# Expert weights of an MoE block, loaded with four neighbouring rows for each partition

## The chip, the cores and the metric

The kernel runs on one core of a Trainium2 chip, as one program. The metric is the time of the program on the device in microseconds. The core's engines are PE (matrix products; PEld is its weight load), DVE (vector), ACT (scalar), POOL and SP, which here only issues DMA transfers. On-chip memory has 128 partitions; a load is described by how many bytes in a run it puts into each partition.

## What is computed

One block of a diffusion backbone, on 512 tokens of 1024 features (and 256 context tokens that only warm up a recurrence): a norm with adaptive shift and scale, two mixers side by side (a gated linear recurrence and a long-convolution head group), an output projection, and then the part that takes most of the time, a mixture of 32 experts with two experts for each token. Last comes a norm. Cut to what matters here:

```
mod = silu(c) @ w_ada + b_ada          # six rows of 1024: shift, scale, gate, twice
x   = x + g1 * (concat(rmsnorm(ya), rmsnorm(yb)) @ w_out)
h   = rmsnorm(x, norm2_g) * (1 + sc2) + sh2
g   = softmax(h @ w_rg + b_rg)         # 4 groups, the best one is taken
e   = softmax over the 8 experts of that group of (h @ w_re + b_re), the best 2
for e in 32 experts:                   # combine[:, e] is 0 for tokens without e
    y   = (silu(h @ w_gate[e]) * (h @ w_up[e])) @ w_down[e]   # 1024 -> 512 -> 1024
    out = out + combine[:, e] * y
x   = rmsnorm(x + g2 * out, final_g)
```

The weights w_gate and w_up of an expert are 1024 x 512 numbers of 4 bytes, w_down is 512 x 1024; each matrix is 2 MB.

## The kernel before, in words

The function `tile_block_kernel` doesn't issue instructions as it goes. Its calls are recorded in a `Recorder`, and for nearly the whole program a planner (`order`, `forward`, `backward`) sorts them before anything is issued: it simulates every engine with a cost for each instruction, takes the ready one of highest priority, and repeats this 24 times with priorities from the pass before. A transfer costs it `nbytes / RATE` with a rate of 386 bytes a nanosecond. So the order on all engines follows from the planned times of all of them, and a changed cost in one stage can change the order in another.

The work comes in stages. Until some 300 us the mixers and the modulation rows run (loads of w_ada, w_in, w_out; products on PE; scans and convolutions on DVE and ACT). From 300 to 358 us come the output projection, the second norm and the routing. For the routing each block of 128 tokens `r` of the residual `x2` is transposed in eight pieces of 128 features into `h2T`, and multiplied with the router's weights `wrA`. For the gather three bf16 tiles `xp[0..2]` are made, which together hold the fp32 value: a copy scaled by the norm's `rs`, the remainder `rem` (what the copy's rounding left), its copy, and the remainder of that. Blocks 0 and 1 get theirs in the loop over `r` (DVE, or ACT where the planner finds it sooner); blocks 2 and 3 after it, the first step on ACT.

Then the experts. They are ranked by their number of tokens. The list `CAPS` gives each rank a fixed number of rows (64, 64, 64, 192, 128, 128, 96, nine times 64, fifteen times 32, and 0 for the last; a loop behind takes what doesn't fit). 31 experts are loaded, the first three (`NPRE`) by their own number before the routing is known. Units pack up to 128 rows: one with two experts of 64, or four experts of 32 (a "quad"). The last unit is such a quad. In `expert_units` a unit gathers its rows by products with 0/1 matrices (bf16, on `xp`), scaled and shifted into `XT` with the features on the partitions, and then `product` multiplies with the gate, up and down weights in fp32; for a quad, four experts stand beside each other, each in 32 columns of the array. The gated result `sg` is transposed into `HT` (features on the partitions again) for the down product, whose two column halves of 512 (the last in two quarters, `LASTP`, in the last unit) are scattered back onto `x2`.

The weights come in 186 loads of 1 MB: for each expert six, gate, up and down (`m`), two halves each (`h`). All are issued by SP, in a fixed order (`chain`), into a ring of 16 buffers of 8 KB a partition (some lie in the "arena", some in "slots", so one tensor has both names in the trace). A load waits until the last product that reads the buffer's old content is done. `wpart` says what a load reads. Before, it is

```
w = w[:, 512 * h:512 * h + 512] if m == "d" else w[512 * h:512 * h + 512]
return w.rearrange("(k p) n -> p k n", p=128)
```

so partition p gets the rows p, 128 + p, 256 + p and 384 + p, each 512 numbers or 2 KB in a run: 512 runs a load. Half h of gate and up are 512 of the 1024 rows; half h of down are 512 of the 1024 columns, with all 512 rows. A product takes the features in the same order as the weight's rows: step k multiplies features 128k to 128k + 127.

Helpers at the top of the file issue all recorded instructions, so that in the trace nearly all of them have the line L565 or L572 (L1822 for the expert loads).

## Time and profile before

| | before |
|---|---|
| median of three runs | 866.7 us (864.5 to 866.82) |
| own time of the profiled execution | 867.37 us |
| span of the profiled execution | 865.6 us |
| PE busy | 798.3 us, 92% of the span |
| DVE, ACT busy | 493.2 us, 279.4 us |
| moved by DMA | 259.71 MB, mean 300 GB/s |
| share of the chain that ended last | PE 64%, DMA 6%, DVE 4% |

The span is what the profiler sees between the first and the last instruction; the program's own time has 1.8 us around it. A share of busy time is a mean over stages; the page also cuts the span into 40 slices, and there PE is near full from the second slice on to the last four, and DMA from 440 us on. A DMA share slightly above 1 means that all 16 engines are full. The list of DMA packets says which run lengths there are: 112966 of 118025 are shorter than 8 KB.

### The profile page before, as it was taken

What the parts mean: (1) busy time and instruction counts of PE and PEld (TensorE: products, weight loads), DVE (VectorE), ACT (ScalarE), POOL (GpSimd) and SP (SyncE); (2) the same over time, 40 slices, a digit from 0 to 9 for tenths busy, and PEclk for the clock granted to TensorE, in tenths of its full rate; (3) what the DMA queues carried; (4) which work ended last, traced back from release to release, by engine and by line L of the source; (5) the groups of instructions that cost most, each with busy time, mean ns of one, the idle gap of its engine ahead of it and who ended that gap; (6) DMA issues with size and microseconds to landing.
All of it is one profiled execution on the core that took longest, in us unless ns stands there. A gap on an engine that the chain in (4) does not pass through costs nothing.

```text
span 865.6 us, 13258 instructions
## 1 busy us (share of the span) xinstructions
PE 798.3 (92%) x5218; PEld 441.1 (51%) x5219; DVE 493.2 (57%) x966; ACT 279.4 (32%) x505; POOL 6.7 (1%) x16
## 2 busy tenths in 40 slices
PE   1969999999998999699999999999999999999774
PEld 0336653587887778553545344444643435345222
DVE  7999967999999988813332332342422144233215
ACT  4688387944353325511102011011110111011005
POOL 0000000000000000000000000000000000000002
PEclk9998999999999999799999999999999999999988
DMA  8953669425221495789899999999999999999993
GB/s 280 415 205 122 226 218 419 158 78 191 73 98 61 163 388 215 255 311 368 292 388 386 387 387 385 387 385 387 386 386 387 387 387 386 386 386 386 387 376 132
DMA packets 118025, 259.71 MB, mean 300 GB/s; under 512 B 6672, under 2 KB 11792, under 8 KB 112966
## 3 DMA queue, kind: packets, MB, share of 16 engines
q1 hardware_dynamic: 117942, 258.80, 81.5%
q8 instruction: 42, 0.69, 0.3%
q14 instruction: 25, 0.20, 0.1%
q10 hardware_dynamic: 16, 0.02, 0.0%
HBM read 252.49 MB, written 6.31 MB: 299 GB/s over the span
## 4 chain that ended last, share of the span: by engine, by line
PE 64%; DMA 6%; DVE 4%; ACT 1%; issue 0%; ACTq 0%; DVEq 0%
PE bank L565 64%; DMA arena<-in_w_up_dram 3%; DMA slot<-in_w_down_dram 2%; DVE arena L565 1%; DVE arena L572 1%; DVE slot L572 1%; DMA slot<-in_w_out_dram 1%; ACT slot L565 1%; DVE slot L565 0%; DVE R L565 0%; ACT arena L565 0%; ACT slot L572 0%; DVE fine L565 0%; DVE finy L565 0%; DVE he L565 0%
## 5 line engine op out<-in xcount | busy, mean ns | idle before, releaser
L565 PE MATMUL bank<-arena 128*64 128x512 f32 (+7 forms) x1314 | 301.3, 558 | 27.5 <-ACT arena L565 14.2
L565 PE MATMUL bank<-slot 128*128 128x512 f32 x968 | 258.6, 411 | 9.8 <-ACT arena L565 2.9
L565 PEld LDWEIGHTS bank<-slot 128*128 128x128 f32 x968 | 177.7, 190 | 91.1 <-issue 27.2
L565 PE MATMUL bank<-slot,arena 128*32 128x512 f32 (+2 forms) x1088 | 208.5, 598 | 4.7 <-DMA slot<-in_w_ada_dram 2.0
L565 PEld LDWEIGHTS bank<-arena 128*64 128x64 f32 (+4 forms) x1314 | 107.2, 139 | 160.0 <-issue 103.4
L565 DVE TENSOR_TENSOR arena<-arena,bank 128x512 f32<-128x512 f32 (+2 forms) x131 | 80.4, 664 | 135.3 <-PE bank L565 135.1
L572 DVE TENSOR_TENSOR arena<-arena 128x512 f32<-128x512 f32 (+3 forms) x139 | 116.6, 870 | 5.5 <-DMA arena<-in_w_dram 3.0
L565 ACT ACTIVATE arena<-bank 128x512 f32<-128x512 f32 (+1 forms) x62 | 36.0, 597 | 235.2 <-PE bank L565 233.3
L565 PEld LDWEIGHTS bank<-slot,arena 128*32 128x32 f32 (+1 forms) x1088 | 52.2, 119 | 97.9 <-issue 81.6
L565 PEld LDWEIGHTS <-slot 128*128 128x128 bf16 x1344 | 78.2, 99 | 27.2 <-issue 26.7
L565 PE MATMUL bank<-R,slot 128*128 128x128 bf16 x1344 | 86.5, 222 | 0.7 <-DVE R L565 0.6
L572 DVE TENSOR_SCALAR arena<-bank,A2c,B2c 128x128 f32<-128x128 f32 x42 | 16.8, 409 | 119.6 <-PE bank L565 119.5
L565 ACT ACTIVATE slot<-arena 128x512 fp32r<-128x512 f32 (+3 forms) x47 | 31.8, 679 | 108.0 <-DVE arena L565 95.5
L572 ACT ACTIVATE arena<-bank,B2c,A2c 128x128 f32<-128x128 f32 x70 | 28.1, 455 | 115.2 <-DVE arena L572 93.1
L565 DVE SCALAR_TENSOR_TENSOR arena<-bank,iw,arena 128x512 f32<-128x512 f32 (+1 forms) x29 | 21.2, 732 | 46.1 <-PE bank L565 45.9
L565 PE MATMUL bank<-ident,arena 128*128 128x128 f32 (+2 forms) x234 | 37.9, 281 | 5.6 <-DVE arena L565 4.3
L565 ACT ACTIVATE arena<-arena 128x512 f32<-128x512 f32 (+6 forms) x59 | 32.9, 591 | 22.1 <-DVE arena L565 16.9
L565 PEld LDWEIGHTS bank<-ident,arena 128*128 128x128 f32 (+2 forms) x234 | 29.5, 156 | 18.5 <-DVE arena L565 9.1
L572 ACT ACTIVATE slot<-slot 128x1024 fp32r<-128x1024 f32 (+1 forms) x33 | 27.6, 862 | 27.5 <-DVE slot L572 15.3
L572 DVE TENSOR_TENSOR slot<-slot 128x1024 fp32r<-128x1024 f32 (+1 forms) x36 | 34.7, 985 | 0.0
L565 ACT ACT_TABLE_LOAD x21 | 26.9, 1283 | 4.6 <-DMA arena<-in_pack_dram 4.2
L565 DVE TENSOR_TENSOR arena<-bank,arena 128x512 f32<-128x512 f32 (+1 forms) x42 | 27.5, 681 | 0.6 <-PE bank L565 0.5
(169 smaller groups left out, 388.9 us busy)
## 6 DMA issues: line engine op xcount, KB each, us to landing
slot<-in_w_gate_dram SPq DMA_DIRECT2D x34, 1024.0 KB, 13.8
arena<-in_w_down_dram SPq DMA_DIRECT2D x34, 1024.0 KB, 14.0
arena<-in_w_up_dram SPq DMA_DIRECT2D x32, 1024.0 KB, 14.0
slot<-in_w_up_dram SPq DMA_DIRECT2D x30, 1024.0 KB, 14.2
arena<-in_w_gate_dram SPq DMA_DIRECT2D x28, 1024.0 KB, 13.5
slot<-in_w_down_dram SPq DMA_DIRECT2D x27, 1024.0 KB, 14.2
slot<-in_w_ada_dram SPq DMA_DIRECT2D x24, 1024.0 KB, 8.4
slot<-in_w_in_dram SPq DMA_DIRECT2D x8, 1024.0 KB, 4.8
```

The lines of the kernel that those rows point to most:

```text
L565: return self.rec.add(self.name, lambda: f(*[real(v) for v in args], **{k: real(v) for k, v in kw.items()}), outs, ins, cost, **x)
L572: return cost, lambda: f(*[real(v) for v in args], **{k: real(v) for k, v in kw.items()}), port
```

## The change

`wpart` now reads four neighbouring rows for a partition, `"(p k) n -> p k n"` with k of 4. For gate and up these are 8 KB in a run: partition p gets the rows 4p to 4p + 3 of the half, in 128 runs a load. Step k of the product then takes the features k, k + 4, k + 8, ... of a half of 512, so all that brings features onto partitions counts by fours: the transposes of `x2`, of the modulation rows `mr` and of `sg` read every fourth column, `xp` and `rem` are written so that a plane's block holds every fourth feature (in two pieces of 512), and the norm's gain `n2` and the router's weights `wr` are packed accordingly. For down a half is now two of a partition's four rows, all 1024 columns wide, again 8 KB in a run, and no longer 512 columns: the tile is cut as `(k c n)` with two rows and two column halves, and `expert_units` takes row step k from half `k // 2`. Both loads of an expert's w_down are needed for its first column half, and both are read until its second. In the last group, whose last load comes in two pieces, the down loads keep column halves (`cols=True`), in runs of 2 KB. The planner gets 0.92 of the bytes for all loads with the long runs.

```diff
+    def fours(v):
+
+        return v.reshape(2, 128, 4, -1).transpose(1, 0, 2, 3).reshape(128, -1)
+
...
@@ -1106,7 +1110,8 @@
-            T.transpose(b[:, 128 * q:128 * q + 128], mr[:, 128 * q:128 * q + 128], ident)
+
+            T.transpose(b[:, 128 * q:128 * q + 128], mr[:, q::4] if g else mr[:, 128 * q:128 * q + 128], ident)
...
+    def four(v):
+        return v.rearrange("s (p q) -> s q p", q=4)
+
+    def fours(v):
+        return v.rearrange("s (q p) -> s q p", q=4)
...
-                    k = 4 * kb + q
-                    T.transpose(b[:, q * 128:(q + 1) * 128], x2[:, r, k * 128:(k + 1) * 128], ident)
+                    T.transpose(b[:, q * 128:(q + 1) * 128], x2[:, r, 512 * kb + q:512 * kb + 512:4], ident)
...
-            X.copy(xp[0][:, r], x2[:, r], scale=rs)
-            V.scalar_tensor_tensor(rem, x2[:, r], rs, xp[0][:, r], op0=OP.mult, op1=OP.subtract)
+            for j in range(2):
+                xj, pj = four(x2[:, r, 512 * j:512 * j + 512]), fours(xp[0][:, r, 512 * j:512 * j + 512])
+                X.copy(pj, xj, scale=rs)
+                V.scalar_tensor_tensor(fours(rem[:, 512 * j:512 * j + 512]), xj, rs, pj, op0=OP.mult, op1=OP.subtract)
...
-        S.activation(rem, x2[:, r], AF.Copy, scale=rss[r % 2])
+        for j in range(2):
+            js = slice(512 * j, 512 * j + 512)
+            S.activation(fours(rem[:, js]), four(x2[:, r, js]), AF.Copy, scale=rss[r % 2])
...
-    def wpart(m, h, w):
-
-        w = w[:, 512 * h:512 * h + 512] if m == "d" else w[512 * h:512 * h + 512]
-        return w.rearrange("(k p) n -> p k n", p=128)
+    def wpart(m, h, w, cols=False):
+
+        if m == "d":
+            w = w.rearrange("(p k) n -> p k n", k=4)
+            if cols:
+                return w[:, :, 512 * h:512 * h + 512]
+            return w[:, 2 * h:2 * h + 2].rearrange("p k (c n) -> p k c n", c=2)
+        return w[512 * h:512 * h + 512].rearrange("(p k) n -> p k n", k=4)
...
-                o = REC.add("SP", go, [dst[:, :, c0:c0 + cols]], [eid[0:1, s:s + 1]] if s >= NPRE else [],
-                            540 if new else 60, nbytes=2048 * cols)
+                    se = wpart(m, h, se, bool(pieces))
+                    return nc.sync.dma_start(out=dst.ap(), in_=se[:, :, c0:c0 + cols] if pieces else se)
+
+                o = REC.add("SP", go, [dst], [eid[0:1, s:s + 1]] if s >= NPRE else [], 540 if new else 60,
+                            nbytes=2048 * cols * (1.0 if pieces else 0.92))
...
-                T.transpose(b[:, q * n:q * n + n], sg[:n, q * 128:(q + 1) * 128], ident[:n, :n])
+                T.transpose(b[:, q * n:q * n + n], sg[:n, q::4], ident[:n, :n])
...
-                b = product(sub, "d", HT[j], [(k, k, h) for k in range(4)], c0, m)
+                b = product(sub, "d", HT[j], [(k, k, h) if last else (k, 2 * (k % 2) + h, k // 2) for k in range(4)], c0, m)
...
-                load(*t, LASTP if gi == len(groups) - 1 and t == todo[-1] and m == "d" else ((0, 512),))
+                load(*t, None if gi < len(groups) - 1 or m != "d" else LASTP if t == todo[-1] else ((0, 512),))
```

The order of the instructions on every engine is the planner's, and it changes throughout. Three places of it follow; in them L569, L576 and L1845 are the same helpers' lines after the change as L565, L572 and L1822 before.

On PE in the middle of the last unit, before the change: `128x512` products are scatters (`bank<-slot`) of the unit before, `32x512` ones are one expert's share of a product of the last quad.

```order
L565 MATMUL bank_73<-slot 128x512
L565 MATMUL bank_67<-slot 128x512
L565 MATMUL bank_68<-slot 128x512
L565 MATMUL bank_71<-arena 32x512
L565 MATMUL bank_70<-slot 128x512
L565 MATMUL bank_71<-arena 32x512
L565 MATMUL bank_67<-slot 128x512
L565 MATMUL bank_68<-slot 128x512
L565 MATMUL bank_74<-slot 128x512
L565 MATMUL bank_69<-slot 128x512
```

After the change, the same place:

```order
L569 MATMUL bank_69<-slot,arena 32x512 x8
L569 MATMUL bank_71<-slot 128x512
L569 MATMUL bank_74<-slot 128x512
L569 MATMUL bank_67<-slot 128x512
L569 MATMUL bank_72<-slot 128x512
L569 MATMUL bank_69<-slot,arena 32x512 x6
L569 MATMUL bank_69<-arena 32x512 x2
L569 LDWEIGHTS R_137
L569 MATMUL bank_70<-combP,R_137 32x3
L569 MATMUL bank_69<-arena 32x512 x14
```

Before, single 32-row products stand between the scatters; after, they come in runs of 8, 8 and 14 (`combP` belongs to the placing of a unit's rows).

On SP around 300 us, where the last loads of the mixers meet the first of the experts: `w_out` is the output projection's weights, `x` the tokens, `gd` a scratch tensor of the filters. Before:

```order
L565 DMA slot<-in_w_out_dram 128x2048
L565 DMA arena<-in_x_dram 128x1024 x2
L565 DMA slot<-in_w_out_dram 128x2048
L565 DMA arena<-in_x_dram 128x1024
L1822 DMA arena<-in_w_gate_dram 128x4x512 x2
L565 DMA arena<-in_x_dram 128x1024
```

And after:

```order
L569 DMA slot<-in_w_out_dram 128x2048
L569 DMA arena<-gd 128x4x256 x2
L569 DMA slot<-in_w_out_dram 128x2048
L569 DMA arena<-in_x_dram 128x1024 x3
L1845 DMA arena<-in_w_gate_dram 128x2048 x2
L569 DMA arena<-in_x_dram 128x1024
```

The pieces of `gd` now stand between the two halves of `w_out`, and three blocks of `x` in a row go ahead of the first expert loads.

On DVE in the second norm, where the planes of a block are made (`hy` is a block's 1/rms, `slot<-arena,hy` the scaled copy, `arena<-arena,hy,slot` the remainder). Before:

```order
L565 TENSOR_TENSOR hy_101<-hy_101,he_103 128x1
L565 TENSOR_TENSOR he_102<-he_102,hv_98 128x1
L572 TENSOR_SCALAR slot<-arena,hy_101 128x1024
L565 TENSOR_SCALAR he_102<-he_102 128x1
L565 SCALAR_TENSOR_TENSOR arena<-arena,hy_101,slot 128x1024
L565 SCALAR_TENSOR_TENSOR arena<-bank_72,rsby_126,arena 128x512
L565 TENSOR_TENSOR hy_100<-hy_100,he_102 128x1
L572 CAST slot<-arena 128x1024
```

And after:

```order
L569 TENSOR_TENSOR hy_101<-hy_101,he_103 128x1
L569 RECIPROCAL hy_100<-hy_100 128x1
L576 TENSOR_SCALAR slot<-arena,hy_101 128x512
L569 TENSOR_TENSOR he_102<-hy_100 128x1
L569 SCALAR_TENSOR_TENSOR arena<-arena,hy_101,slot 128x512
L569 SCALAR_TENSOR_TENSOR arena<-bank_68,rsby_126,arena 128x512
L569 TENSOR_TENSOR he_102<-he_102,hv_98 128x1
L569 SCALAR_TENSOR_TENSOR arena<-arena,hy_101,slot 128x512
L569 SCALAR_TENSOR_TENSOR arena<-bank_71,rsby_126,arena 128x512
L569 TENSOR_SCALAR he_102<-he_102 128x1
L569 TENSOR_TENSOR hss_97<-sx_129 128x1
```

One copy of 1024 features and one remainder of 1024 are now pieces of 512, and instructions of the other block and of the residual (`rsby`) stand between them.

## Rows read from the trace of the kernel before

**Rows 1.** the page, part 1: busy time, share and instructions of each engine
```profile
PE 798.3 (92%) x5218; PEld 441.1 (51%) x5219; DVE 493.2 (57%) x966; ACT 279.4 (32%) x505; POOL 6.7 (1%) x16
```

**Rows 2.** windows: length, busy us (instructions) of each engine, granted clock, DMA share, GB/s
```profile
200.00:300.00 100.00, 95.72 (x443) 79.17 (x443) 97.41 (x117) 40.44 (x63) 0.00 (x0) 1.00 0.32 110
440.00:600.00 160.00, 159.81 (x1181) 74.21 (x1183) 55.50 (x108) 21.34 (x43) 0.00 (x0) 1.00 1.05 386
600.00:800.00 200.00, 199.31 (x1657) 91.92 (x1653) 65.81 (x127) 27.06 (x55) 0.00 (x0) 1.00 1.05 386
806.00:850.00 44.00, 32.39 (x208) 10.72 (x209) 10.67 (x19) 5.98 (x13) 1.69 (x2) 0.92 0.94 345
```

**Rows 3.** the chain that ended last: start us, us, engine or transfer
```profile
358.80 75.03 PE bank L565 x603
...
810.78 14.01 DMA arena<-in_w_up_dram
824.84 4.94 PE bank L565 x21
...
843.81 6.29 PE bank L565 x60
```

**Rows 4.** waits of PE, 806 to 850 us: total us, times, longest
```profile
PE bank L565 <- DMA arena<-in_w_up_dram: 5.0, 3, 1.7
PE bank L565 <- DMA arena<-in_w_down_dram: 1.7, 1, 1.7
PE bank L565 <- DMA slot<-in_w_up_dram: 1.5, 1, 1.5
PE bank L565 <- DMA slot<-in_w_down_dram: 1.1, 1, 1.1
```

**Rows 5.** windows, five us in the last unit
```profile
825.00:830.00 5.00, 5.00 (x25) 1.02 (x22) 0.00 (x0) 0.00 (x0) 0.00 (x0) 0.50 1.05 387
```

**Rows 6.** windows in which w_ada and w_in are loaded
```profile
26.00:36.00 10.00, 9.45 (x42) 4.18 (x44) 9.94 (x17) 6.11 (x12) 0.00 (x0) 1.00 1.01 417
138.00:148.00 10.00, 9.24 (x50) 2.90 (x52) 5.53 (x8) 7.85 (x11) 0.00 (x0) 1.00 1.02 419
```

**Rows 7.** line L1822 (the expert loads): from issue to landing
```profile
DMA to landing us min/median/max: 5.3/14.0/15.8
```

**Rows 8.** timeline of SP, 715 to 740: start us, us, line, operation, count
```profile
722.24 9.68 SPq L1822 DMA_DIRECT2D arena<-in_w_gate_dram  x4
733.50 2.53 SPq L1822 DMA_DIRECT2D slot<-in_w_gate_dram  x2
```

**Rows 9.** timeline of PE, three places: x counts passes, two for an fp32 product
```profile
749.94 3.64 PE L565 MATMUL bank<-slot,arena 128*32 128x512 f32 x32
753.40 1.04 PE L565 MATMUL bank<-arena 128*32 128x512 f32 x8
...
802.42 1.04 PE L565 MATMUL bank<-arena 128*32 128x512 f32 x2
803.40 0.49 PE L565 MATMUL bank<-slot 128*128 128x512 f32 x1
```

**Rows 10.** timeline of DVE in the mixers, out<-in and their shapes
```profile
50.31 0.69 DVE L572 TENSOR_TENSOR slot<-arena,slot 128x512 fp32r<-128x512 f32 x1
...
75.86 1.14 DVE L572 TENSOR_TENSOR slot<-arena,slot 128x512 fp32r<-128x512 f32 x1
```

**Rows 11.** timeline of ACT in the mixers
```profile
48.49 0.68 ACT L572 ACTIVATE slot<-arena 128x512 fp32r<-128x512 f32 x1
...
75.63 1.19 ACT L572 ACTIVATE slot<-arena 128x512 fp32r<-128x512 f32 x1
```

**Rows 12.** timeline of DVE before the experts
```profile
339.07 0.75 DVE L572 TENSOR_SCALAR slot<-arena,hy 128x1024 bf16<-128x1024 f32 x1
...
339.85 1.28 DVE L565 SCALAR_TENSOR_TENSOR arena<-arena,hy,slot 128x1024 f32<-128x1024 f32 x1
```

**Rows 13.** timeline of ACT before the experts
```profile
350.58 2.19 ACT L565 ACTIVATE arena<-arena,hy 128x1024 f32<-128x1024 f32 x2 [1.01 <-DVE hy L565]
```

More of the change, by code (lines that the diff above doesn't have):

```diff
@@ L106, in lay @@
     wr = np.concatenate([i["w_rg"][0], i["w_re"][0], np.zeros((D, 28), np.float32)], axis=1)
-    small = {"c": cols(i["c"]), "cc": cols(i["c_ctx"]), "n1": cols(i["norm1_g"]), "n2": cols(i["norm2_g"]), "fb1": twice(i["filt_b1"].T),
+    small = {"c": cols(i["c"]), "cc": cols(i["c_ctx"]), "n1": cols(i["norm1_g"]), "n2": fours(i["norm2_g"].reshape(D, 1)), "fb1": twice(i["filt_b1"].T),
              "ff1": twice(i["filt_freq1"].T), "fb2": twice(i["filt_b2"].T), "ff2": twice(i["filt_freq2"].T), "fw1": i["filt_w1"][0],
@@ L111, in lay @@
              "cbw": cols(i["conv_b_w"]), "ga": cols(i["out_norm_a"]),
[L112 removed]
+             "gb": cols(i["out_norm_b"]), "wr": fours(wr),
              "brb": np.broadcast_to(np.concatenate([i["b_rg"], i["b_re"]], axis=1), (128, 36)),
@@ L1803, with load @@
     regs, chain, owner = {}, [], {}
-    def load(s, m, h, pieces=((0, 512),)):
+    def load(s, m, h, pieces=None):
         src = wsrc[m]
@@ L1810, in load @@
             nring[0] += 1
-            dst = t[:, :].rearrange("p (k n) -> p k n", k=4)
-            for c0, cols in pieces:
+            wt[s, m, h] = t.rearrange("p (k n) -> p k n", k=4), (nring[0] - 1) % NW
+            for c0, cols in pieces or ((0, 512),):
+                if m == "d" and not pieces:
+                    dst = t.rearrange("p (k c n) -> p k c n", k=2, c=2)
+                else:
+                    dst = wt[s, m, h][0][:, :, c0:c0 + cols]
                 new = s >= NPRE and s not in regs
@@ L1816, in load, with go @@
                     regs[s] = None
-                def go(dst=dst[:, :, c0:c0 + cols], c0=c0, cols=cols, new=new):
+                def go(dst=dst, c0=c0, cols=cols, new=new):
                     if new:
@@ L1821, in go @@
                     se = src[s] if s < NPRE else src[ds(regs[s], 1)].rearrange("o k n -> (o k) n")
-                    return nc.sync.dma_start(out=dst.ap(), in_=wpart(m, h, se)[:, :, c0:c0 + cols])
-                o = REC.add("SP", go, [dst[:, :, c0:c0 + cols]], [eid[0:1, s:s + 1]] if s >= NPRE else [],
-                            540 if new else 60, nbytes=2048 * cols)
+                    se = wpart(m, h, se, bool(pieces))
+                    return nc.sync.dma_start(out=dst.ap(), in_=se[:, :, c0:c0 + cols] if pieces else se)
+                o = REC.add("SP", go, [dst], [eid[0:1, s:s + 1]] if s >= NPRE else [], 540 if new else 60,
+                            nbytes=2048 * cols * (1.0 if pieces else 0.92))
                 if chain:
@@ L2011 @@
                     for h in range(2):
-                        t = ring[len(wo)].rearrange("p (k n) -> p k n", k=4)
+                        t = ring[len(wo)]
                         se = wsrc[m][ds(e, 1)].rearrange("o k n -> (o k) n")
-                        SP.dma_start(out=t, in_=wpart(m, h, se))
-                        wo[m, h] = t
+                        wo[m, h] = t.rearrange("p (k n) -> p k n", k=4)
+                        SP.dma_start(out=t.rearrange("p (k c n) -> p k c n", k=2, c=2) if m == "d" else wo[m, h],
+                                     in_=wpart(m, h, se))
                 def wks(m, k, h):
```

2 lines of the change are left out of this document (removed).

## The prediction

> **What bounds the kernel now.** I read four views in this order. The page's first part says that PE is busy for 798.3 of 865.6 us [rows 1]; that average hides stages with different limits, so the windows come next. In them [rows 2] PE is idle 4.3 us from 200 to 300. From 440 to 800 us two resources run side by side without a gap: PE is busy 159.81 of 160 and 199.31 of 200 us, and the DMA engines show a share of 1.05 at 386 GB/s all the time. From 806 to 850 PE falls to 32.39 of 44 us, while the stream runs on at full share until its last load (0.94 over the stretch). The chain of waits says what that means [rows 3]: its last steps alternate between short bursts of PE and 14-us transfers of up and down weights, so in the last unit the stream of weights sets the end, and what follows the last load is 6.29 us of PE and the final norm. The waits table gives the size: PE waits 5.0 + 1.7 + 1.5 + 1.1 = 9.3 us for weights there [rows 4]. It pays a second time: after the idle stretch it runs 825 to 830 at a granted clock of 0.50, the lower of its levels (1.2 of 2.4 GHz), busy 5.00 of 5.00 us, which is 2.5 us more than the same work at full clock [rows 5].
>
> So before 806 PE sets the pace (DMA only keeps the ring of 16 buffers full, and waits for PE to free one), and after it DMA does. A faster stream helps at the end only, by as much as it can run ahead.
>
> **Part 1: 8 KB runs for the expert loads.** Each load moves 1 MB. With its present 2 KB runs the stream makes 386 GB/s [rows 2], so 1.0486 MB / 386 = 2.716 us a load. The same trace has transfers with 8 KB runs, those of w_ada and w_in, at stretches in which DMA is just as full: 417 and 419 GB/s at shares of 1.01 and 1.02 [rows 6]. At 419 a load takes 2.503 us, 0.214 us less. I take that value; the lower end is no gain, if those stretches owe their rate to something else.
>
> The Trainium skill ("DMA: Bandwidth & Descriptors", section "Why small descriptors are slow (HBM only)") puts a fixed cost of about 3 cycles on each packet of 32-byte beats: my estimate from it is 67/64 against 259/256 cycles, 3.5%, or 0.09 us a load. The rows show 8.5%, and I go by them; by the page's rule the 6.4 us below would be 2.7 us, and the time some 4 us higher.
>
> How far may the stream run ahead? Load by load until it has no more free buffer. The tightest place is at 733.5 us, where SP, whose previous issue ended at 722.24 + 9.68 = 731.92, waits until PE frees a buffer [rows 8]. From issue to landing a load takes 14.0 us at the median and 5.3 at least [rows 7]: up to 8.7 us of it is standing in the queue, and 1.6 us of this is already used at that place (733.50 - 731.92). So the stream can get 7.1 us ahead up to there, and no more however fast it is. Behind that place follow 38 loads (counted in the trace to the last issue; some 2.7 us each), of which the last 8, the down halves of the last four experts, keep their 2 KB runs; the other 30 gain 30 x 0.214 = 6.4 us. Without a ring the bound would be the whole stretch at 386 GB/s, 440 to 820 us or 140 loads: 0.214 x 140 = 30 us.
>
> The down halves of an expert are now its upper and lower rows (of the contraction) and no longer its left and right columns. Both must have landed before the first product, and the first half is read until the middle of the second product: a half product of a 32-row unit is 3.46 us (749.94 to 753.40, [rows 9]), so its buffer comes free 1.7 us later. Up to 800 us the loads land far enough ahead that the first effect costs nothing (PE waits for no weights there: 359.1 of 360 us busy); without that cover it would cost one load, 2.7 us. The second I charge in full: 1.7 us.
>
> **Part 2: the new order on PE.** The planner gets 0.92 of the bytes for these loads and sorts everything anew. Fp32 products of 32-row units use a quarter of the array each, and four run beside each other. A run of four steps takes 3.46 us, 0.86 a step; a single one in between occupies 802.42 to 803.40, 0.98 us, for a quarter of the work [rows 9]. In the order of before, 19 of 59 such runs have a length that is no multiple of four, and they need 158 steps; of after 4 of 58, 148 steps. Ten steps at 0.86 are 8.6 us less PE. Six of them lie before the tight place, 5.2 us, and there buffers come free that much earlier; the other four lie in the last unit, beside DMA waits. The order is the planner's, so if the chip delays one input the gain at that spot goes: lower end 0.
>
> **Part 3: the stride of four.** The transposes, and the copies and remainders that feed the gather's planes, now read every fourth feature (16 bytes apart), and row blocks are done in two pieces of 512. That is on the path: from 339 us to the start of the experts at 358.80 [rows 3] DVE works on the planes and the routing, and the experts wait for both. For blocks 0 and 1 a TENSOR_SCALAR of 0.75 us and a SCALAR_TENSOR_TENSOR of 1.28 us are split [rows 12]; a split costs some 0.10 us (twice 0.69 for 512 elements [rows 10] against 1.28 for 1024), so 0.2 a block. ACT's part for blocks 2 and 3, 2.19 us for both [rows 13], is split too. No row shows a strided read alone. The nearest are two instructions of the mixers' convolutions: where read and write both step 16 bytes, a TENSOR_TENSOR of 512 takes 1.14 us, where both step 8 bytes 0.69, and an ACTIVATE that writes at 16 bytes 1.19 against 0.68 [rows 10, 11]. So the ends: at nothing for the stride, 2 x 0.2 = 0.4 us; at the full 0.45 for each of four pieces a block, 2 x (0.2 + 1.8) = 4.0 us, and 4 x 0.51 = 2.0 us more if all of ACT's part shows, 6.0 us. I take the middle, 3.2 us, since the nearest row has two strided sides where here is one. PE's strided transposes I cost at nothing: in the second norm PE waits for DVE beside them; in the units they have no cover, and no row prices them.
>
> **Part 4: the order before the experts.** On SP the loads of w_out, x and the filters change places. Nothing in the first 300 us does more work. What an order can win or lose there is the 4.3 us of PE idle between 200 and 300 us [rows 2]: 0, with ends -4.3 and +4.3.
>
> **The sum**, against the profiled execution's own 867.4 us (the median of the runs is 866.7, so 0.7 us come off at the end). Stream: -7.1 - 5.2 + 1.7 - 6.4 = -17.0 us. PE, if no weights were late: -9.3 - 2.5 - 8.6 = -20.4 us. The smaller gain is the one that counts, so the stream is still last in the final unit, with some 3 us of waits left. Plus 3.2 for the strides: 867.4 - 17.0 + 3.2 = 853.6, and 0.7 less on the scale of the median: forecast 853 us.
>
> **The rivals.**
> (a) PE becomes the only bound: the stream gains more at the tight place, as more of the 30 us reach the end, and no weight is late. Then 867.4 - 20.4 - 0.7 = 846 us with the strides at nothing, 849 with them. For it: -17.0 and -20.4 are near each other. Against: SP stands waiting for buffers already.
> (b) The order's gain doesn't come: 867.4 - 17.0 + 5.2 + 3.2 - 0.7 = 858 us. For it: the planner's times are not the chip's. Against: single steps are plainly dear [rows 9].
> (c) The front and the routing slip: 853 + 4.3 + 2.8 (strides at their upper end) = 860 us. For it: DVE is busy 97.41 of 100 us before the routing [rows 2], so a shift there has no slack to fall into. Against: nothing there does more work.
> (d) Slower: the rate stays 386 GB/s, since it belongs to these tensors or to the steady state and not to the run length. Then the buffers that come free sooner buy nothing at the end, all of the last unit's waits remain, the stream starts late by the strides' 3.2 us because its buffers are freed later, and a down product waits for a second half, up to 2.7 us: 867.4 + 3.2 - 0.7 + (0 to 2.7) = 870 to 873 us. It decides when the gain per load times the loads behind the tight place is under the strides' price, 3.2 / 30 = 0.107 us a load, that is under 402 GB/s, and the queue's slack is not used. Against: 417 and 419 GB/s [rows 6].
> The Trainium skill (same page, section "Where 436 GB/s comes from") lets HBM bind loads into SBUF at some 358 GB/s for a core, by which the run length couldn't matter and (d) would hold; the trace disagrees with its 386 and 419 on one core, so (d) gets little.
>
> **How the numbers follow.** Forecast 0.43 (848 to 857), (a) 0.20, (b) 0.17, (c) 0.12, (d) 0.08. A measurement of this kernel tells 0.3% from no change, 2.6 us: faster means under 864.1, slower over 869.3. Forecast, (a), (b) and most of (c) are faster, 0.89; same 0.04, the high tail of (c) and low tail of (d); slower 0.07. The range of 8 in 10 leaves out (d) and the outer tails of (a) and (c): 844 to 863.
>
> **What would show it.** In the profile after, 440 to 800 us shows under 2.0 us of PE idle and a DMA rate that is over 386 wherever SP doesn't wait, and its packets are 8 KB; SP waits for buffers longer and oftener; issue to landing falls below 14.0 at the median; PE's waits for weights after 800 us fall from 9.3 to some 3 us and the half-clock stretch goes; the routing's chain on DVE grows by 0.4 to 6.0 us. I am wrong if the loads land 2.7 us apart where the queue is full, if a new wait for down weights stands before 800 us, or if the experts start over 5 us later than 358.8.

## The result, and the profile after

The changed kernel takes 856.25 us (median of 4 runs, 855.16 to 856.57) against 866.36 us before: a ratio of 0.9886, with a 95% interval of 0.9873 to 0.9898. It is faster by 10.1 us; 13.7 us were forecast. (Measured once more, with experiment 9: 859.86 against 867.1 us.) The profiled execution has a span of 854.7 us against 865.6.

The page's first part and the DMA line of its second, after: PE is 11 us less busy, and there are 49673 packets in place of 118025.

```profile
PE 787.1 (92%) x5218; PEld 441.4 (52%) x5219; DVE 496.1 (58%) x965; ACT 281.1 (33%) x505; POOL 18.0 (2%) x21
...
DMA packets 49673, 259.71 MB, mean 304 GB/s; under 512 B 6672, under 2 KB 11792, under 8 KB 21830
```

The windows that answer to [rows 2], in the same columns; the last is the stretch of the last unit, 44 us as before:

```profile
200.00:300.00 100.00, 95.79 (x443) 79.29 (x442) 94.77 (x112) 37.69 (x61) 7.10 (x2) 0.99 0.32 111
440.00:600.00 160.00, 160.00 (x1193) 75.15 (x1186) 53.17 (x101) 19.40 (x38) 0.00 (x0) 1.00 1.01 415
600.00:800.00 200.00, 199.51 (x1701) 93.67 (x1698) 69.44 (x135) 30.04 (x61) 0.00 (x0) 1.00 0.98 398
796.00:840.00 44.00, 34.89 (x232) 13.19 (x229) 13.46 (x24) 7.62 (x18) 3.07 (x3) 1.00 0.89 339
```

From 440 to 600 us the stream moves 415 GB/s in place of 386, and PE stays full. From 600 to 800 us the share has fallen to 0.98: DMA now has idle time in the middle of the stage. Where it lies, three windows of 5 us show:

```profile
715.00:720.00 5.00, 5.00 (x43) 2.46 (x41) 1.00 (x2) 0.00 (x0) 0.00 (x0) 1.00 0.58 202
...
735.00:740.00 5.00, 5.00 (x39) 2.11 (x38) 3.75 (x10) 1.86 (x3) 0.00 (x0) 1.00 0.66 233
740.00:745.00 5.00, 5.00 (x36) 2.82 (x35) 4.57 (x8) 0.01 (x1) 0.00 (x0) 1.00 1.00 419
```

PE is full in all three; DMA has 0.58 and 0.66 of its time in two. It waits for buffers. SP's timeline answers to [rows 8]:

```profile
730.30 0.99 SPq L1845 DMA_DIRECT2D slot<-in_w_gate_dram  x2
737.72 0.90 SPq L1845 DMA_DIRECT2D arena<-in_w_up_dram  x2
```

The first load of the second row was issued at 738.65 us before and landed 13.1 us later; now it is issued at 737.72, and it lands 4.7 us later, at 742.4 (the landing from its semaphore in the trace). From 700 to 775 us SP waits for PE for 56.0 us in 13 waits, after, and for 31.2 us in 19 waits before: longer, as predicted, but not oftener. The waits of SP (total, times, longest), after:

```profile
SPq L1845 <- PE bank L569: 56.0, 13, 7.8
```

The same view of the kernel before:

```profile
SPq L1822 <- PE bank L565: 31.2, 19, 4.0
```

The chain that ended last, for [rows 3] (start, us, what ran or was moved):

```profile
362.76 9.61 PE bank L569 x105
...
778.28 15.30 DMA slot<-in_w_gate_dram
793.70 19.91 DMA arena<-in_w_up_dram
813.65 3.25 PE bank L569 x26
816.90 15.71 DMA slot<-in_w_down_dram
832.65 6.50 PE bank L569 x61
```

The chain has the same shape as before. The end is still set by transfers of up and down weights, and the last burst of PE starts at 832.65 in place of 843.81. The experts start at 362.76 in place of 358.80. PE's waits in the last unit, for [rows 4], are 7.7 us against 9.3:

```profile
PE bank L569 <- DMA slot<-in_w_down_dram: 3.2, 3, 1.7
PE bank L569 <- DMA arena<-in_w_up_dram: 2.3, 2, 1.5
PE bank L569 <- DMA arena<-in_w_down_dram: 1.7, 1, 1.7
...
PE bank L569 <- DMA slot<-in_w_up_dram: 0.5, 1, 0.5
```

The half-clock stretch of [rows 5] is gone: from 796 to 840 us the granted clock is 1.00 (the last window above), also in the least busy five us there:

```profile
820.00:825.00 5.00, 2.14 (x14) 0.33 (x14) 0.00 (x0) 0.00 (x0) 0.00 (x0) 1.00 1.05 388
```

From issue to landing, for [rows 7]:

```profile
DMA to landing us min/median/max: 4.7/13.3/20.7
```

Before the experts, a copy of 512 on DVE takes 0.70 us where one of 1024 took 0.75 [rows 12], a remainder of 512 1.18 where one of 1024 took 1.28, and ACT's four pieces 4.48 where two whole ones took 2.19 [rows 13]. DVE's timeline, after:

```profile
341.80 0.70 DVE L576 TENSOR_SCALAR slot<-arena,hy 128x512 bf16<-128x512 f32 x1
...
342.54 1.18 DVE L569 SCALAR_TENSOR_TENSOR arena<-arena,hy,slot 128x512 f32<-128x512 f32 x1
```

ACT's timeline, after:

```profile
355.39 4.48 ACT L569 ACTIVATE arena<-arena,hy 128x512 f32<-128x512 f32 x4 [1.01 <-DVE hy L569]
```

To say where time went, the span is cut at two instructions on DVE that every version has: the first sum of squares of the second norm (`hss<-sx`), and the mask of the chosen experts (`Mb<-arena`). Before:

```profile
337.32 0.16 DVE L565 TENSOR_TENSOR hss<-sx 128x1 f32<-128x1 f32 x1 [0.19 <-ACT arena L565]
...
355.56 0.29 DVE L565 TENSOR_TENSOR Mb<-arena 128x128 bf16<-128x128 f32 x1
```

After:

```profile
339.83 0.16 DVE L569 TENSOR_TENSOR hss<-sx 128x1 f32<-128x1 f32 x1
...
360.38 0.29 DVE L569 TENSOR_TENSOR Mb<-arena 128x128 bf16<-128x128 f32 x1
```

So the front until the norm takes 2.5 us longer (339.83 - 337.32), the norm and the routing 2.3 us longer (20.55 against 18.24), and from the mask to the end of the span the kernel is 15.7 us shorter (854.7 - 360.38 = 494.3 against 510.0). 2.5 + 2.3 - 15.7 = -10.9, the difference of the spans.

### The profile page after: what moved, and what is told of

It is laid out like the page before. It is cut to its first block, busy times and chain, and to the rows that moved or that the text cites. A ratio compares the mean times of both kernels' runs of the same rounds, so it can differ in the third digit from the quotient of the medians.

```text
span 854.7 us, 13256 instructions
## 1 busy us (share of the span) xinstructions
PE 787.1 (92%) x5218; PEld 441.4 (52%) x5219; DVE 496.1 (58%) x965; ACT 281.1 (33%) x505; POOL 18.0 (2%) x21
## 2 busy tenths in 40 slices
DMA packets 49673, 259.71 MB, mean 304 GB/s; under 512 B 6672, under 2 KB 11792, under 8 KB 21830
## 4 chain that ended last, share of the span: by engine, by line
PE 71%; DVE 8%; DMA 7%; ACT 3%; issue 1%; POOL 0%; DVEq 0%; ACTq 0%; SPq 0%
PE bank L569 71%; DVE arena L576 4%; DMA arena<-in_w_up_dram 2%; DVE slot L576 2%; DMA slot<-in_w_down_dram 2%; DMA slot<-in_w_gate_dram 2%; DVE arena L569 1%; ACT arena L569 1%; DMA slot<-in_w_in_dram 1%; ACT slot L576 1%; ACT slot L569 1%; ACT arena L576 0%; DVE slot L569 0%; POOL slot L576 0%; DVE he L569 0%
## 5 line engine op out<-in xcount | busy, mean ns | idle before, releaser
L569 PE MATMUL bank<-arena 128*64 128x512 f32 (+8 forms) x1314 | 294.7, 553 | 23.7 <-ACT arena L569 9.8
L569 PE MATMUL bank<-slot 128*128 128x512 f32 x968 | 253.4, 407 | 11.3 <-DVE arena L576 3.0
L569 PEld LDWEIGHTS bank<-slot 128*128 128x128 f32 x968 | 176.8, 189 | 85.3 <-issue 12.3
L569 PE MATMUL bank<-slot,arena 128*32 128x512 f32 (+2 forms) x1088 | 205.4, 599 | 4.0 <-DMA slot<-in_w_down_dram 3.2
L569 PEld LDWEIGHTS bank<-arena 128*64 128x64 f32 (+5 forms) x1314 | 106.6, 139 | 151.7 <-issue 103.7
L569 DVE TENSOR_TENSOR arena<-arena,bank 128x512 f32<-128x512 f32 (+2 forms) x131 | 80.4, 663 | 86.7 <-PE bank L569 86.5
L576 DVE TENSOR_TENSOR arena<-arena 128x512 f32<-128x512 f32 (+3 forms) x137 | 116.6, 885 | 7.3 <-ACT arena L569 3.9
L569 PEld LDWEIGHTS bank<-slot,arena 128*32 128x32 f32 (+1 forms) x1088 | 51.1, 118 | 100.1 <-issue 81.1
L569 PEld LDWEIGHTS <-slot 128*128 128x128 bf16 x1344 | 78.6, 100 | 24.5 <-issue 23.9
L569 ACT ACTIVATE arena<-bank 128x512 f32<-128x512 f32 (+1 forms) x62 | 35.9, 596 | 161.6 <-PE bank L569 160.0
L569 PE MATMUL bank<-R,slot 128*128 128x128 bf16 x1344 | 86.2, 223 | 0.0
L576 DVE TENSOR_SCALAR arena<-bank,A2c,B2c 128x128 f32<-128x128 f32 x45 | 17.8, 409 | 105.7 <-PE bank L569 105.6
L576 ACT ACTIVATE arena<-bank,B2c,A2c 128x128 f32<-128x128 f32 x67 | 27.4, 456 | 155.2 <-PE bank L569 84.7
L569 ACT ACTIVATE slot<-arena 128x512 fp32r<-128x512 f32 (+3 forms) x47 | 31.8, 678 | 122.1 <-DVE arena L569 119.5
L569 DVE SCALAR_TENSOR_TENSOR arena<-bank,iw,arena 128x512 f32<-128x512 f32 (+1 forms) x29 | 21.2, 732 | 75.4 <-PE bank L569 74.5
L569 PE MATMUL bank<-ident,arena 128*128 128x128 f32 (+2 forms) x234 | 38.4, 286 | 9.2 <-DVE arena L569 7.8
L569 PEld LDWEIGHTS bank<-ident,arena 128*128 128x128 f32 (+2 forms) x234 | 32.7, 184 | 21.7 <-DVE arena L569 6.3
L576 ACT ACTIVATE slot<-slot 128x1024 fp32r<-128x1024 f32 (+1 forms) x31 | 25.4, 848 | 45.6 <-DVE slot L576 24.2
L569 ACT ACTIVATE arena<-arena 128x512 f32<-128x512 f32 (+6 forms) x59 | 32.8, 591 | 21.7 <-DVE arena L569 16.9
L576 DVE TENSOR_TENSOR slot<-slot 128x1024 fp32r<-128x1024 f32 (+1 forms) x35 | 33.2, 973 | 1.2 <-ACT slot L576 1.0
L569 DVE TENSOR_TENSOR R<-iota,rk 128x256 bf16<-128x256 f32 (+1 forms) x33 | 11.3, 355 | 38.6 <-PE bank L569 38.5
L569 DVE TENSOR_TENSOR arena<-bank,arena 128x512 f32<-128x512 f32 (+1 forms) x42 | 27.5, 680 | 1.6 <-PE bank L569 1.5
```

What stands on the lines that cost most here:

```text
L569: return self.rec.add(self.name, lambda: f(*[real(v) for v in args], **{k: real(v) for k, v in kw.items()}), outs, ins, cost, **x)
L576: return cost, lambda: f(*[real(v) for v in args], **{k: real(v) for k, v in kw.items()}), port
```

## The experiments

In what follows "order" means the sequence of instructions on every engine. Where an experiment holds it, the edit changes only what a transfer or a copy reads, and every engine has the same rows as the kernel that it is compared with.

**1. The changed order with 2 KB runs.**

```diff
...
-                    se = wpart(m, h, se, bool(pieces))
-                    return nc.sync.dma_start(out=dst.ap(), in_=se[:, :, c0:c0 + cols] if pieces else se)
+                    if pieces:
+                        return nc.sync.dma_start(out=dst.ap(), in_=wpart(m, h, se, True)[:, :, c0:c0 + cols])
+                    se = se[:, 512 * h:512 * h + 512] if m == "d" else se[512 * h:512 * h + 512]
+                    return nc.sync.dma_start(out=dst.ap(), in_=se.rearrange("(k p) n -> p k n", p=128))
```

> The changed kernel with every instruction of every engine in its changed order, but each expert load again in 512 runs of 2 KB (the rows then don't match the features, so the experts' values are not the reference's). Theory: the run length sets the rate, so the stream is back at 386 GB/s and, as the experts start 4 us later than before and the first buffers come free 9 us later, it ends later than it did before the change: from load 39 on (454.2 us against 448.5) it runs without a gap, 454.2 + 398.2 = 852.4 us for the last landing against 846.7, so 868 to 872 us. Rival 1, the gain is the ten steps that the new order saves on PE and not the runs: 856 to 858 us. Rival 2, the runs alone made the whole gain and the order cost nothing: 865 to 867 us.

Measured 878.0 us, ratio 1.014 (1.0116 to 1.0164): slower than the kernel before, and by more than expected. Its PE isn't full any more in the middle of the stage. The window from 600 to 700 us:

```profile
600.00:700.00 100.00, 90.75 (x730) 42.64 (x724) 27.46 (x54) 12.37 (x25) 0.00 (x0) 0.97 1.05 386
```

PE's waits from 440 to 700 us:

```profile
PE bank L569 <- DMA slot<-in_w_gate_dram: 5.4, 1, 5.4
PE bank L569 <- DMA arena<-in_w_up_dram: 3.3, 2, 1.7
PE bank L569 <- DMA slot<-in_w_up_dram: 0.5, 1, 0.5
```

The stream is at 386 GB/s and full, and the new order asks for weights sooner than it brings them: 9.2 us of waits where before had 0.2. The runs, with the order held, are worth 856.25 - 878.0 = -21.8 us (-18.1 by the changed kernel's second measurement, 859.86). Both rivals fall.

**2. The old order with 8 KB runs.** Nothing is strided, and no product waits for a second half. The down loads of the last group stay at 2 KB (`long` is false for them).

```diff
...
-                    return nc.sync.dma_start(out=dst.ap(), in_=wpart(m, h, se)[:, :, c0:c0 + cols])
+                    if not long:
+                        return nc.sync.dma_start(out=dst.ap(), in_=wpart(m, h, se)[:, :, c0:c0 + cols])
+                    if m == "d":
+                        se = se.rearrange("(p k) n -> p k n", k=4)[:, 2 * h:2 * h + 2]
+                    else:
+                        se = se[512 * h:512 * h + 512].rearrange("(p k) n -> p k n", k=4)
+                    return nc.sync.dma_start(out=dst.ap(), in_=se)
...
```

> The kernel before with every instruction in its old order, but the expert loads in 128 runs of 8 KB (down as two of a partition's four rows; the last group's down loads stay at 2 KB); nothing is strided and no product waits for a second half (the rows don't match the features, so the experts' values are not the reference's). Theory: the stream runs at 420 GB/s until the buffers run out at 733 to 772 us, where PE's releases, unchanged, hold it: load 163 is issued at 773.4 us as before and lands some 7 us after it instead of 13.5, and the 23 loads behind it gain 1.5 to 3 us: 866.4 - 8.0 to 9.5 = 857 to 858.5 us, all of the change's gain but 1 to 2 us. Rival 1, the saved steps on PE are the gain: 864 to 867 us. Rival 2, the rate is the gain and the strides cost 3 to 4 us of it: 852 to 854 us.

Measured 853.86 us, ratio 0.9854 (0.9837 to 0.9871). The run length alone gives 12.6 us (866.44 - 853.86), more than the whole change. That is in rival 2's bounds and 3 us under my theory's. The theory took PE's releases as unchanged; but the load that it named, issued at 773.4 us before, is issued at 770.0 here. The windows show the stream at 420 GB/s and then held back:

```profile
440.00:500.00 60.00, 60.00 (x504) 28.30 (x504) 21.69 (x45) 7.83 (x16) 0.00 (x0) 1.00 1.01 420
...
700.00:770.00 70.00, 69.32 (x633) 32.12 (x629) 27.92 (x57) 9.96 (x20) 0.00 (x0) 1.00 0.89 347
```

**3. Planes read and written in line**, in the changed order.

```diff
-                xj, pj = four(x2[:, r, 512 * j:512 * j + 512]), fours(xp[0][:, r, 512 * j:512 * j + 512])
+                xj, pj = x2[:, r, 512 * j:512 * j + 512], xp[0][:, r, 512 * j:512 * j + 512]
...
-            S.activation(fours(rem[:, js]), four(x2[:, r, js]), AF.Copy, scale=rss[r % 2])
+            S.activation(rem[:, js], x2[:, r, js], AF.Copy, scale=rss[r % 2])
```

> The changed kernel in its own order, but the copies and remainders that make the gather's planes (blocks 0 to 3, still two pieces of 512 each) read and write neighbouring features; the router's transposes keep the stride, so the routing is unchanged (the experts get features in another order than the weights, so their values are not the reference's). Theory: each SCALAR_TENSOR_TENSOR of 512 falls from 1.18 to about 0.74 us and each strided copy on DVE from 0.70 to about 0.40, so the experts start 2 to 3 us sooner, PE frees every buffer that much sooner, and since buffers hold the stream, the end comes 2 to 3 us sooner: 853 to 854.5 us. Rival, the stream's own rate holds the end and the start has slack: 856 us. Second rival, the strided read costs nothing and the late start comes from the new order: DVE durations unchanged, 856 us.

Measured 854.15 us (852.79 to 859.29), ratio 0.9871 (0.9847 to 0.9896). The interval doesn't tell it from the changed kernel, but its trace gives the price. The same two instructions on DVE's timeline:

```profile
343.19 0.49 DVE L576 TENSOR_SCALAR slot<-arena,hy 128x512 bf16<-128x512 f32 x1
...
343.71 0.75 DVE L569 SCALAR_TENSOR_TENSOR arena<-arena,hy,slot 128x512 f32<-128x512 f32 x1
```

And ACT's four pieces:

```profile
354.82 2.56 ACT L569 ACTIVATE arena<-arena,hy 128x512 f32<-128x512 f32 x4 [1.01 <-DVE hy L569]
```

A read at 16 bytes costs 1.18 against 0.75 us for the remainder, 0.70 against 0.49 for the copy, and 4.48 against 2.56 for ACT's four. The stretch from the norm to the mask falls from 20.55 to 18.58 us.

**4. Pairs in place of fours** for gate and up, two runs of 4 KB, in the changed order.

```diff
-        return w[512 * h:512 * h + 512].rearrange("(p k) n -> p k n", k=4)
+        return w[512 * h:512 * h + 512].rearrange("(a p b) n -> p a b n", a=2, b=2)
...
-        return v.rearrange("s (p q) -> s q p", q=4)
+        return v.rearrange("s (p q) -> s q p", q=2)
```

> The changed kernel in its own order with pairs in place of fours for gate and up: two runs of 4 KB for each partition, features counted by twos (8 bytes apart) in the transposes, copies and remainders; down loads as in the changed kernel. All of the reference is computed. Theory: gate and up loads run at some 400 to 410 GB/s, which costs little, since buffers and not the rate hold the stream until 770 us (the 15 loads behind it lose 0.07 us each, 1 us); an 8-byte stride reads at the plain price, so the experts start 2 to 3 us sooner as in the kernel with planes in line: 854 to 855.5 us. Rival, the rate counts over the whole stretch: 0.07 us x 90 gate and up loads behind 440 us = 6 us less, 859 to 860 us after the sooner start. Second rival, a stride of two costs as much as one of four: 857 us.

Measured 856.95 us (852.32 to 859.71), ratio 0.9885 (0.9861 to 0.991). By its time it can't be told from the change; that is the second rival's number (a stride of two as dear as one of four), but the trace shows that its reason is wrong. It tells two things. On DVE's timeline the remainder at 8 bytes takes what the one in line took:

```profile
346.82 0.75 DVE L569 SCALAR_TENSOR_TENSOR arena<-arena,hy,slot 128x512 f32<-128x512 f32 x1
```

And in a window in which it is full the stream makes 413 GB/s:

```profile
440.00:500.00 60.00, 60.00 (x624) 33.58 (x618) 21.94 (x46) 8.97 (x21) 0.00 (x0) 1.00 1.02 413
```

The time that the stride gave back went into the front: here the norm's first sum is at 344.33 us, 4.5 us later than in the changed kernel's profile, with the same order. So the front of this order isn't steady from run to run; experiment 9 takes this up.

**5. The change with the planner's bytes at 1.0.**

```diff
-                            nbytes=2048 * cols * (1.0 if pieces else 0.92))
+                            nbytes=2048 * cols * 1.0)
```

> The changed kernel with the planner's bytes at 1.0 for all expert loads in place of 0.92: the layout of fours as in the change, but another sort, whose 32-row products need 157 steps (148 with 0.92, 158 before). All of the reference is computed. Theory: the runs of 8 KB are the gain, and the ten steps are worth next to nothing, since the new sort gives them back in a later start of the experts: with the strides' 2 us on top of the 853.9 us of the old order with 8 KB runs, 855 to 858 us. Rival, the ten steps are worth 8.6 us as I counted: 863 to 865 us.

Measured 864.54 us, ratio 0.9981 (0.9968 to 0.9994). My theory falls, the rival's number holds: the same layout in a sort of 157 steps loses nearly all of the gain. Yet experiment 2, with 158 steps, was at 853.86. As the table below shows, the two differences have different places: against experiment 2 the experts start 7 us later (mask at 361.73 against 354.68), and against the changed kernel the stage behind the mask is 7 us longer.

**6. The kernel before with 0.92** for the same loads; they stay at 2 KB.

```diff
-                            540 if new else 60, nbytes=2048 * cols)
+                            540 if new else 60, nbytes=2048 * cols * (0.92 if long else 1.0))
```

> The kernel before with only the planner's bytes at 0.92 for the loads that the change lengthens: the new kind of sort (148 steps), and the loads in 2 KB runs as ever; nothing is strided. All of the reference is computed. Theory: an order that counts on a stream 8% faster meets one that isn't, and PE waits for weights in the middle of the stage, as it did for 16 us with the changed order and 2 KB runs: 868 to 877 us. Rival, the steps saved are a gain of their own: 858 to 862 us.

Measured 864.93 us, ratio 0.9984 (0.9975 to 0.9994): neither of the two. This sort saves the steps too, and starts early (mask at 353.60), but from the mask to the end it takes 510.7 us, as before. PE waits from 440 to 700 us for weights, 4.6 us:

```profile
PE bank L565 <- DMA slot<-in_w_down_dram: 2.9, 2, 1.7
PE bank L565 <- DMA arena<-in_w_up_dram: 1.7, 1, 1.7
```

So saved steps buy nothing while the stream is slow.

**7 and 8. Pairs with whole planes**, at 1.0 and at 0.96. The copies and remainders are again single instructions of 1024 (all even features of a block, then all odd ones; the gather takes its blocks accordingly).

```diff
-            for j in range(2):
-                xj, pj = four(x2[:, r, 512 * j:512 * j + 512]), fours(xp[0][:, r, 512 * j:512 * j + 512])
-                X.copy(pj, xj, scale=rs)
...
+            xj, pj = four(x2[:, r]), fours(xp[0][:, r])
+            X.copy(pj, xj, scale=rs)
...
-                            nbytes=2048 * cols * (1.0 if pieces else 0.92))
+                            nbytes=2048 * cols * (1.0 if pieces else 0.96))
```

> Pairs in place of fours for gate and up (runs of 4 KB, features counted by twos), down as in the change, and the planes' copies and remainders of blocks 0 and 1 and ACT's of blocks 2 and 3 again in one piece of 1024; the planner's bytes at 1.0. The order until the experts is then that of before (its first 2181 PE instructions are the same), behind it 157 steps. All of the reference is computed. Theory: the start of the experts as before (nothing strided that costs, the old front), the stream at some 411 GB/s, held by buffers anyway: the 853.9 us of the old order with 8 KB runs plus 0 to 1.5 us, 854 to 855.5 us. Rival, the rate counts over the whole stretch: 0.055 us x 140 loads = 8 us more, 861 to 862 us.

> The same kernel of pairs with the planner's bytes at 0.96, nearer to the rate of 4 KB runs: 149 steps, and an order before the experts that follows the old one for the first 642 PE instructions only. All of the reference is computed. Theory: if its experts start about where they did before (358 us), the saved steps show at last: 850 to 853 us; if they start 3 to 5 us later, as in the changed kernel, 854 to 857 us. Rival, the steps are worth nothing wherever they stand: the same as with 1.0.

Measured at 1.0: 856.35 us, ratio 0.9892 (0.9877 to 0.9907), 1 us above what I expected. At 0.96: 851.93 us, ratio 0.9832 (0.9817 to 0.9847), as expected of an early start. Both start early (masks at 354.33 and 354.76), so the 4.4 us between them are the second sort's, with eight steps fewer and a fast stream. The second is faster than the kernel before and than the change.

**9. Fours with whole planes**, at 1.0 and at 0.96, in the orders of 7 and 8; **and the changed kernel once more**.

> Fours as in the change (runs of 8 KB), but the planes' copies and remainders in one piece of 1024, and the planner's bytes at 1.0. Every engine's order is then that of the kernel of pairs at 1.0 (856.35 us), whose first 2181 PE instructions are those of before. All of the reference is computed. Theory: what makes the changed kernel's experts start late, beside the strides, is the order of the front that the planner finds for the split pieces; with the old front only the strides' 2 us are left against the pairs, and the stream at 420 in place of 411 GB/s gives back at most 1 us: 857 to 858.5 us. Rival, the late front comes with the stride itself and not with the split: 862 to 865 us, as with fours in two pieces at 1.0.

> The same kernel of fours in one piece with the planner's bytes at 0.96: every engine's order is that of the kernel of pairs at 0.96 (851.93 us). All of the reference is computed. Theory: the strides' 2 us show in full in the start of the experts, and the faster stream gives back 0 to 1 us: 853 to 854 us. Rival, with the saved steps the stream is what is late, so 420 in place of 411 GB/s counts for 0.055 us on each of the 70 to 140 loads: 846 to 850 us.

> The changed kernel itself once more, for a second profiled execution of its front: the three kernels that share its order had the mask of the chosen experts (Mb on DVE) at 359.8 to 363.9 us, the kernel before at 355.6. Theory: the late front belongs to this order: 360 to 364 us again, and a time of 855.5 to 858 us. Rival, the 360.4 us of the first profile were chance: 356 to 358 us.

Measured at 1.0: 857.59 us (854.05 to 859.13), ratio 0.9888 (0.9867 to 0.9909), as expected of the strides alone, against 864.54 with split planes (experiment 5). At 0.96: 852.41 us (849.35 to 854.18), ratio 0.9836 (0.9819 to 0.9852), no different from pairs; the rival's 846 to 850 us didn't come. The changed kernel again: 859.86 us (855.92 to 860.33) with the kernel before at 867.1 beside it, ratio 0.9903 (0.9883 to 0.9923). That is over the 855.5 to 858 us that I expected, and the mask is over its 360 to 364 us too; the rival (356 to 358) falls. The second profile has the norm and the mask 5 us later than the first:

```profile
344.62 0.16 DVE L569 TENSOR_TENSOR hss<-sx 128x1 f32<-128x1 f32 x1
...
365.53 0.29 DVE L569 TENSOR_TENSOR Mb<-arena 128x128 bf16<-128x128 f32 x1
```

All profiled executions, cut at the two instructions on DVE; each number is a start in the trace or a difference of two, in us. Each row is one execution, and two of them are far from the median of their runs: that of 2 took 856.18 us (median 853.86), that of 9 at 0.96 took 849.35 (median 852.41).

| kernel | order: steps | run | until norm | norm to mask | mask to end |
|---|---|---|---|---|---|
| before | 158 | 2 KB | 337.3 | 18.2 | 510.0 |
| 2 | as before | 8 KB | 336.4 | 18.2 | 499.7 |
| 6 | 148 | 2 KB | 335.4 | 18.2 | 510.7 |
| change, first and second | 148 | 8 KB | 339.8, 344.6 | 20.6, 20.9 | 494.3, 492.9 |
| 1 | as the change | 2 KB | 343.3 | 20.6 | 514.1 |
| 3 | as the change | 8 KB, planes in line | 341.2 | 18.6 | 492.3 |
| 4 | as the change | 4 KB | 344.3 | 18.6 | 493.0 |
| 5 | 157, split planes | 8 KB | 341.2 | 20.6 | 501.6 |
| 7 | 157 | 4 KB | 335.9 | 18.4 | 499.6 |
| 8 | 149 | 4 KB | 336.4 | 18.4 | 495.8 |
| 9 at 1.0 | as 7 | 8 KB | 334.5 | 20.5 | 498.9 |
| 9 at 0.96 | as 8 | 8 KB | 334.1 | 20.6 | 492.9 |

## Why the prediction came out as it did

The direction and the range were right, and the mechanism that carries the gain is shown. The forecast was 3 us too low, and its terms were further off than their sum; that they nearly cancelled is luck. By the steps of the sum:

**The rate (-7.1 - 6.4 = -13.5).** The mechanism is shown: with the old order held, longer runs take the stage from the mask to the end from 510.0 to 499.7, -10.3 us (the medians of the runs give -12.6). The stream makes 420 GB/s where it is full, as I took from w_ada and w_in (419). The 7.1 us of slack in the queue were used, and a little more: the load that landed 13.1 us after its issue now lands 4.7 us after it. The term that was mis-sized is the 30 loads behind the tight place at 0.214 us each. In the changed kernel the 27 loads from the one issued at 737.72 to the last up load take 71.2 us from landing to landing against 73.0 before, 1.8 us less in place of 5.8. I had taken one tight place; SP waits for buffers again and again from 700 to 775 us. (By the trace 29 loads stand there and not 30, as the eight down halves take nine issues; that is 0.2 us.)

The sentence on the Trainium skill ("DMA: Bandwidth & Descriptors", section "Why small descriptors are slow (HBM only)") gets its answer too. The windows show 386, 413 and 420 GB/s at 2, 4 and 8 KB: 7% more where two thirds of the loads have 4 KB, and 8.8% at 8 KB. My estimate from the page's 3 cycles a packet was 3.5% for the second. The measurement decides: longer runs gained more here than that overhead gives. What else makes up the difference, no run shows.

**The order on PE (-5.2 + 1.7 before the end).** With runs of 8 KB, the changed order takes 494.3 (492.9 in the second profile) where the old one takes 499.7: -5.4 to -6.8 us, in place of the -3.5 that I charged. This rests on the one profile of experiment 2, whose execution took 2.3 us more than its median; if those lie in this stage, the order is worth -3.1 to -4.5. With runs of 2 KB the same order costs +4.1 (514.1 against 510.0), and the other order of 148 steps gains nothing (510.7, experiment 6). So the two parts of the change don't add: in these runs the saved steps paid only with the faster stream. I had written the order's gain down as releases of buffers, and as a lower end 0; a loss, from weights asked for too early, was missing. That PE would be left with 3 us of waits was wrong too: 7.7 us stayed, as the stream gained less behind the tight place than I had charged, while PE's busy time fell by 11.2 us.

**The strides (+3.2).** From the norm to the mask 2.3 us: 2.0 are the strides, shown by taking them away (20.55 to 18.58) and once more between experiments 7 and 9 in the same order (18.39 to 20.54), and 0.3 go with the split pieces and their order (18.24 to 18.58). The two strided rows that the term was taken from belong to the first norm, where its output is split in two parts, and not to the convolutions; their 0.45 us for 512 elements was near the 0.43 of the remainder here. The Trainium skill ("SBUF — State Buffer", section "Door 1: The DMA port swizzle (why `[64,N]` ≈ `[32,N]`)", on cachelines of 16 bytes) asks for two hits in a line for the full rate. The rows agree: fp32 at 8 bytes has two and costs nothing (0.75 us a remainder), at 16 bytes it has one, and a remainder costs 0.43 us more. The page also gives four fp32 as the step that is still free; this case doesn't bear that out.

**The front (0, with ends -4.3 and +4.3).** This is the step that failed. The first profile's +2.5 us lies inside my ends, the second's +7.3 doesn't. In the second the experts start at 367.91 us, 9.1 later than before, and "over 5 us later" was a sign that I had named of being wrong. All five profiles of the changed order have the norm at 339.8 to 344.6 us; the seven of the orders without split planes have it at 334.1 to 337.3. I took the PE idle from 200 to 300 us as the bound; it is 4.2 us now against 4.3 before. PE's busy time until the experts is the same in both kernels too, and what grew are its waits over the whole front (358.80 - 317.03 = 41.8 us before, 362.70 - 316.94 = 45.8 after). The windows up to the experts, before:

```profile
0.00:358.80 358.80, 317.03 (x1508) 218.13 (x1509) 325.73 (x607) 203.44 (x342) 0.79 (x8) 0.98 0.58 212
```

And after:

```profile
0.00:362.70 362.70, 316.94 (x1502) 218.10 (x1503) 325.43 (x598) 204.09 (x342) 12.02 (x13) 0.98 0.56 210
```

Much of that lies between 280 and 320 us, partly behind the stretch that I had looked at. There PE is idle 2.4 us before and 6.9 after, when it waits for ACT and DVE. Before:

```profile
280.00:320.00 40.00, 37.63 (x165) 30.26 (x164) 38.20 (x67) 14.17 (x27) 0.00 (x0) 0.96 0.71 253
```

And after:

```profile
280.00:320.00 40.00, 33.09 (x147) 26.69 (x146) 39.52 (x69) 14.78 (x29) 0.00 (x0) 0.96 0.76 291
```

In the same window it is idle 5.5 to 7.0 us in all six profiles with split planes, and 2.4 to 3.6 us in the seven without.

Experiments 5 and 9 at 1.0 differ in the split of the planes and the sort that comes of it, and in 6.7 us of front. That the split as such, and not the sort that the planner happened to find for it, makes the front late is not shown: the two couldn't be parted with this planner. Why the same order's front varies by 5 us from run to run stays open as well. All of it has come before 223 us: the same three products on DVE start at 222.22 us in the first profile of the changed kernel and at 227.18 in the second, whose chain has a transfer of `gd` of 7.51 us at 194.58 that the first one's doesn't have.

**The rivals.** (a) and (d) fall: the stream is still late in the last unit, and it does run at 420. (b), that the order gives nothing, is wrong where the runs are 8 KB. (c) is the one that came true in part: the front slipped, but the strides stayed under the middle and not at their upper end. For the profiled execution the sum was -17.0 + 3.2 = -13.8 us, measured were -10.9: +2.5 us are the front, -0.9 the strides, and +1.3 the stage behind the mask, in which by the profile of experiment 2 a rate term too large (-13.5 against -10.3) and an order term too small (-3.5 against -5.4) nearly cancel. The split between these two is uncertain by the 2.3 us named above; their sum isn't.

## What to carry to other kernels

Where a stream of weights and PE run side by side through a ring of buffers, count a faster stream as the slack in its queue plus the rate on the loads behind the *last* place at which it waits for a buffer, not the first; this one case speaks for it. When a planner sorts the program, judge a change of layout and the new sort apart: transfer the old order to the new layout (or the reverse) before deciding which of them paid, and look at the stages that the change doesn't touch. And half the run length at half the stride was no worse a trade: 4 KB runs for two thirds of the loads kept nearly all of the rate (413 of 420 GB/s), and 8-byte reads cost nothing (0.75 us a remainder, as in line).

## What the runs showed of the hardware

At full share of the DMA engines, loads of 1 MB moved 386 GB/s in 2 KB runs, 413 with two thirds of them in 4 KB runs, and 420 in 8 KB runs. An issue on SP took 1.8 to 2.4 us at the median (0.37 us at least) in 2 KB runs and 0.33 us in 8 KB runs. A remainder of 512 fp32 on DVE took 1.18 us when it read at a step of 16 bytes, and 0.75 us at 8 bytes or in line.
